# Every tile that a matmul reads begins on a multiple of 128 bytes, on both sides of SBUF

## The chip, the core and the metric

The kernel runs on one core of a Trainium2 chip. The metric is the device time of one execution in microseconds, the median of several runs; lower is better. Engines are named as in the profile: PE (TensorE, matmuls), PEld (TensorE's weight load), DVE (VectorE), ACT (ScalarE), POOL (GpSimd) and SP (SyncE, which here only issues DMAs).

## What is computed

One layer of an encoder block on 512 positions of width 1024, all in float32. The reference, cut to the core:

```python
n = rms_norm(h, norm_mix_pre[l])
proj = jnp.einsum('bsd,de->bse', n, w_in[l])
z_gmlp, q, k, v, gates = jnp.split(proj, split_points, axis=-1)
y_a = gmlp_spatial_gating(jax.nn.gelu(z_gmlp), ln_v_gain[l], ln_v_bias[l], w_spatial[l], b_spatial[l])
...
o_g, lse_g = dilated_window_attention(q[:, :, sl], k[:, :, sl], v[:, :, sl], dilation, window // (2 * dilation))
...
y_b = jnp.sum(w_mix[..., None] * o_all, axis=0).reshape(B, S, ATTN_GROUP_WIDTH).astype(h.dtype)
g_all = jax.nn.sigmoid((gates + b_gate[l]).astype(jnp.float32)).astype(h.dtype)
merged = (g_a * jnp.einsum('bse,ed->bsd', y_a, w_branch_a[l])
          + g_b * jnp.einsum('bse,ed->bsd', y_b, w_branch_b[l]))
h = h + rms_norm(jnp.einsum('bsd,de->bse', merged, w_out[l]), norm_mix_post[l])
n2 = rms_norm(h, norm_mlp_pre[l])
hid = jnp.square(jax.nn.relu(jnp.einsum('bsd,df->bsf', n2, w_up[l])))
h = h + rms_norm(jnp.einsum('bsf,fd->bsd', hid, w_down[l]), norm_mlp_post[l])
```

The widths: q, k and v have 12 heads of 128 each (three groups of four heads), the gMLP part 2 x 512, the gates 2 x 1024, the hidden layer 4096.

## The kernel before

**Precision.** Almost every product is made of three matmuls. Each float32 operand is split into a rounded part `hi` (type float32r, written by ACT) and the rest `lo` (written by DVE), and `mm3` (lines 83 to 87) adds hi times hi, hi times lo and lo times hi in PSUM. Line 85 is the first of the three, 86 the second, 87 the third. The profile shows float32r as f32. The matmuls that are plain float32 are few: transposes, the scores of groups 1 and 2 (line 307), the values of groups 1 and 2 (line 407), the spatial gating (line 472) and some small ones.

**Operands.** A matmul has a stationary operand, 128 columns loaded beforehand by an LDWEIGHTS (PEld), and a moving operand of up to 512 columns that streams past it. The call is `matmul(out, stationary, moving)`. The profile prints "out<-moving,stationary" or the two in the other order, as the names sort.

**Stages, in order of time.** Norm of x and its transposes into `nh`, `nl` (right side); v of group 0 and of groups 1 and 2 (pv, `token_major`; for groups 1 and 2 the stationary operand takes every fourth position of `nh`); for each of four heads the projections of q and k (pf, `feature_tile`, weights stationary, `nh` and `nl` moving), rotary positions, scores and softmax, and the attention of the head before; the gMLP branch (pv and pf again); the gates and the two branch projections (pf; moving `nh`, `nl`, `yah`, `yal`, `ybh`, `ybl`); the output projection (pd; stationary `mh`, `ml`, moving the weights); post-norm, second norm and transposes; the up projection, whose first four feature tiles are plain (pu) and whose others are made of seven products of half size (line 680, 256 columns; moving `n2` tiles, stationary `hl` and `a12` tiles); the down projection (pd; stationary `hh`, `hl` or, for the last four of 32 steps, `hhl`; moving the weights in `hl` of the pool wback); post-norm and output.

The order of the instructions on each engine is made by the framework's scheduler from the program. All weights come by DMA from SP's queue; POOL's queue has small loads and the residual.

**Where tiles lie.** SBUF has 128 partitions, and a tile takes a range of bytes in each. Pools are stacks: those with no side grow upward from the low end, those with `side="right"` grow downward from the high end. A tile starts at the next multiple of 32 bytes behind the tile before it, so odd sizes shift all that comes behind. The addresses of the kernel before, from its allocation (bytes per partition):

| tiles | read by matmuls as | first address | past a multiple of 128 |
|---|---|---|---|
| ident | moving, in transposes | 16512 | 0 |
| onesq | stationary, 3 products in all | 17184 | 32 |
| small tiles xa, xc | moving, 2 small products a head | 18624, 19456 | 64; 0 and 64 |
| hi, lo of weights (wpool, w0pool, gapool, wopool) | both | 44736 ... | 64 |
| v0h, v0l, v12, mh, ml, hl, a12, hh, ptah, ptal, ptb | both | 69312 ... | 64 |
| perm | stationary | 137920 | 64 |
| q1, k1, q2, k2, q0h, q0l, k0h, k0l (apool, behind perm) | both | 138976 ... | 96 |
| nh, nl | both | 192480, 210912 | 96 |
| ybh, ybl, yah, yal | moving | 159712 ... | 96 |
| n2, hhl (n2pool) | moving; stationary | 172000 ... | 96 |

The slices that matmuls take of these tiles begin at multiples of 512 bytes (256 for `nh` and `nl`) from the tile's start, so a slice has its tile's offset. The exceptions are the slices with a step of four positions (lines 212 to 218), which start up to 12 bytes later.

The offsets on the low side come from the pool `consts` (lines 50 to 61): `ident` 512 bytes, `cols` 128, `neghalf` 8 in a place of 32, `onesq` 512, `warm` 8 in a place of 32, together 1216, which is 64 more than a multiple of 128. The pool `small` behind it takes a multiple of 128. The high end of the right side is 229344, 96 more than a multiple of 128, and `nl` ends there. `perm` has 264 columns, 1056 bytes, 32 more than a multiple of 128.

Of the kernel before, what the change touches and what calls it, by code (L numbers as in the profile page):

```python
# [10 lines left out]
F32 = mybir.dt.float32  # L11
# [5 lines left out]
P = 128  # L17
# [19 lines left out]
def block_kernel(ctx: ExitStack, tc: tile.TileContext, x, norm_mix_pre, w_in, b_gate, ln_v_gain, ln_v_bias,  # L37
                 w_spatial, b_spatial, w_branch_a, w_branch_b, w_out, norm_mix_post, norm_mlp_pre, w_up,
                 w_down, norm_mlp_post, ident_c, rope_c, mask_c, perm_c, out):
    nc = tc.nc  # L40
# [3 lines left out]
    def pool(stack, name, bufs=1, space=None, side=None):  # L44
        kw = {"side": side} if side else {}
        if space is not None:
            kw["space"] = space
        return stack.enter_context(tc.tile_pool(name=name, bufs=bufs, reuse_waits="tile", **kw))

    consts = pool(ctx, "consts")  # L50
# [2 lines left out]
    wpool = pool(wstack, "wpool", bufs=3)  # L53

    ident = consts.tile([P, P], F32, name="ident")
    cols = consts.tile([P, 32], F32, name="cols")
    neghalf = consts.tile([P, 2], F32, name="neghalf")
    onesq = consts.tile([P, P], F32, name="onesq")
    nc.vector.memset(onesq, 1.0)
# [29 lines left out]
    def rstd_of(ss, mult, eps=EPS):  # L89
# [7 lines left out]
        nc.gpsimd.tensor_tensor(r, t, neghalf[:, :1], op=ALU.pow)  # L97
        return r

    right = ExitStack()  # L100
    npool = pool(right, "npool", side="right")
    nh = npool.tile([P, KD, S + ROT], F32R, name="nh")
# [130 lines left out]
    apool = pool(proj, "apool")  # L233
# [1 line left out]
    masks = apool.tile([P, 6, P], F32, name="masks")  # L235
    nc.gpsimd.dma_start(rope, rope_c.rearrange("a p s -> p a s"))
    nc.gpsimd.dma_start(masks, mask_c.rearrange("m p c -> p m c"))
    perm = apool.tile([P, 2 * P + 8], F32, name="perm")
    nc.gpsimd.dma_start(perm, perm_c)
    by_r = perm[:, 2 * P:2 * P + 4].unsqueeze(1).unsqueeze(1)  # L240
    by_c = perm[:, 2 * P + 4:2 * P + 8].unsqueeze(1).unsqueeze(3)

# [185 lines left out]
    nc.gpsimd.dma_start(wsp, w_spatial.rearrange("g t s -> t g s"))  # L428
    pt = psA.tile([P, 32], F32, name="ptr", tag="T")
    nc.tensor.transpose(pt, rows, ident[:32, :32])  # L430
    nc.vector.tensor_copy(cols, pt)
    wst = gpool.tile([P, 4, P], F32, name="wst")
    pt = psA.tile([P, 4, P], F32, name="pt", tag="T")
    for g in range(4):
# [2 lines left out]
    pt = psA.tile([P, 4, P], F32, name="prs", tag="T")  # L437
# [135 lines left out]
    for t in range(4):  # L573
# [14 lines left out]
        for q, hs in enumerate(halves):  # L588
            nc.scalar.activation(xn[:, hs], h2[:, hs], AF.Copy, scale=r)
            pt = psB.tile([P, 4, P], F32, name="pt2", tag="tp", bufs=4)  # L590
# [216 lines left out]
```

## Time and profile before

| | us |
|---|---|
| median of 3 runs | 839.2 |
| lowest and highest | 838.79, 840.05 |
| the profiled execution | 839.99 |
| its span, first to last instruction | 838.2 |

The profile shows one execution. A line of its list of groups reads: source line, engine, operation, output tile, input tiles, shapes and count, then busy time in us and mean duration of one in ns, then idle time of the engine just before these and what ended it. Matmuls are pipelined: the duration of one reaches into the next, so their sum is more than the time that passed, and the distance from one start to the next is the cost of one in a stream. A table of stretches gives for each window its length, the busy time and count of the instructions that run in it (those that began before it too), the clock granted to TensorE, the DMA engines' busy share and GB/s. In the timeline the first column is the start from the beginning of the span, the second the duration, both in us.

### The profile page before, as it was taken

To read this page: it belongs to the slowest core of one execution; us is meant where nothing else is said; L and a number is where in the kernel's file an instruction comes from. 1 tells how busy PE (TensorE), PEld (TensorE's weight loads), DVE (VectorE), ACT (ScalarE), POOL (GpSimd) and SP (SyncE) were. 2 spreads that over 40 slices of the span, in tenths; PEclk is the share of its full clock that TensorE was granted. 3 is DMA by queue.
4 is the path that set the end of the run, shared out by engine and by line. 5 is a ranking of instruction groups with operands and counts; after the bars stand their busy time and mean duration, and the time that the engine had idled before them with its cause. 6 is when DMAs were issued, how large, how long until landed. Compare 5 with 4: busy or idle time off the path is not lost.

```text
span 838.2 us, 10932 instructions
## 1 busy us (share of the span) xinstructions
PE 819.9 (98%) x4371; PEld 707.3 (84%) x4371; DVE 491.4 (59%) x831; ACT 348.6 (42%) x561; POOL 84.5 (10%) x78
## 2 busy tenths in 40 slices
PE   7999999999999999999999989999999999999997
PEld 5899888888888778888888879999999888888885
DVE  6422788978764737443333489989887633333324
ACT  6322243444344444323312465666666632223311
POOL 2100113223224300000000220000000100000000
PEclk9999999999999999999999989999999999999999
DMA  9432233231213233422413242334333722222202
GB/s 295 141 101 79 73 101 101 58 93 55 97 51 90 88 100 126 152 77 74 151 51 100 76 154 73 102 109 132 113 101 126 251 99 87 84 87 97 100 1 100
DMA packets 70373, 86.90 MB, mean 104 GB/s; under 512 B 2034, under 2 KB 57490, under 8 KB 70323
## 3 DMA queue, kind: packets, MB, share of 16 engines
q1 hardware_dynamic: 67810, 77.67, 29.5%
q0 software_dynamic: 2512, 8.54, 3.0%
q8 instruction: 34, 0.56, 0.3%
q14 instruction: 17, 0.13, 0.0%
HBM read 82.01 MB, written 4.19 MB: 103 GB/s over the span
## 4 chain that ended last, share of the span: by engine, by line
PE 96%; ACT 2%; DMA 1%; DVE 1%; issue 0%; SPq 0%; DVEq 0%; POOLq 0%; ACTq 0%
PE pf L87 12%; PE pf L86 12%; PE pf L85 12%; PE pacc L680 11%; PE pd L85 9%; PE pd L86 9%; PE pd L87 9%; PE ptp L680 5%; PE pv L85 4%; PE pv L87 4%; PE pv L86 4%; PE pu L85 1%; PE pu L86 1%; PE pu L87 1%; PE py L407 1%; PE psb L307 1%
## 5 line engine op out<-in xcount | busy, mean ns | idle before, releaser
L87 PE MATMUL pf<-nh,lo 128*128 128x512 f32 x352 | 139.9, 397 | 0.0
L86 PE MATMUL pf<-nl,hi 128*128 128x512 f32 x352 | 139.7, 397 | 0.0
L85 PE MATMUL pf<-nh,hi 128*128 128x512 f32 x352 | 139.5, 397 | 0.0
L680 PE MATMUL pacc<-n,hl 128*128 128x256 f32 x840 | 104.4, 279 | 0.0
L680 PEld LDWEIGHTS pacc<-n,hl 128*128 128x128 f32 x840 | 100.9, 188 | 0.2 <-ACT hl L80 0.2
L85 PE MATMUL pd<-hl,hh 128*128 128x512 f32 x224 | 87.1, 390 | 1.0 <-ACT hh L80 1.0
L86 PE MATMUL pd<-hl,hh 128*128 128x512 f32 x224 | 87.2, 389 | 0.0
L87 PE MATMUL pd<-hl 128*128 128x512 f32 x224 | 86.0, 389 | 0.0
L87 PEld LDWEIGHTS pf<-nh,lo 128*128 128x128 f32 x352 | 66.1, 188 | 15.4 <-issue 0.2
L85 PEld LDWEIGHTS pf<-nh,hi 128*128 128x128 f32 x352 | 66.1, 188 | 15.3 <-issue 0.2
L86 PEld LDWEIGHTS pf<-nl,hi 128*128 128x128 f32 x352 | 66.1, 188 | 15.2
L81 DVE TENSOR_TENSOR hl<-hid,hh 128x512 fp32r<-128x512 f32 x28 | 19.3, 693 | 80.4 <-ACT hh L80 78.9
L248 POOL TENSOR_TENSOR sw<-sw,rope 32x512 f32<-32x512 f32 x24 | 43.9, 1830 | 178.6 <-DVE sw L246 161.2
L80 ACT ACTIVATE hh<-hid 128x512 fp32r<-128x512 f32 x28 | 17.6, 631 | 93.3 <-PE pd L86 93.3
L85 PE MATMUL pv<-hi,nh 128*128 128x512 f32 x128 | 52.0, 410 | 1.1 <-ACT nh L80 1.1
L86 PE MATMUL pv<-lo,nh 128*128 128x512 f32 x128 | 51.9, 405 | 0.0
L87 PE MATMUL pv<-hi,nl 128*128 128x512 f32 x128 | 51.9, 407 | 0.0
L85 PEld LDWEIGHTS pd<-hl,hh 128*128 128x128 f32 x224 | 42.0, 188 | 10.4 <-ACT hh L80 1.4
L87 PEld LDWEIGHTS pd<-hl 128*128 128x128 f32 x224 | 42.0, 188 | 8.7
L86 PEld LDWEIGHTS pd<-hl,hh 128*128 128x128 f32 x224 | 42.0, 188 | 8.6
L97 POOL TENSOR_TENSOR rs_out<-rs_in,neghalf 128x1 f32<-128x1 f32 x20 | 14.7, 734 | 333.7 <-DVE rs_in L94 329.9
L81 DVE TENSOR_TENSOR hl<-dnw,hl 128x1024 fp32r<-128x1024 f32 x32 | 39.2, 1226 | 14.0 <-ACT hl L80 14.0
(243 smaller groups left out, 1568.0 us busy)
## 6 DMA issues: line engine op xcount, KB each, us to landing
upw<-in_w_up_dram SPq DMA_DIRECT2D x16, 1024.0 KB, 5.6
dnw<-in_w_down_dram SPq DMA_DIRECT2D x16, 1024.0 KB, 5.0
qkw<-in_w_in_dram SPq DMA_DIRECT2D x24, 512.0 KB, 4.2
gw<-in_w_in_dram SPq DMA_DIRECT2D x8, 1024.0 KB, 5.2
slab<-in_w_in_dram SPq DMA_DIRECT2D x6, 1024.0 KB, 14.0
wow<-in_w_out_dram SPq DMA_DIRECT2D x4, 1024.0 KB, 4.9
w0raw<-in_w_in_dram SPq DMA_DIRECT2D x4, 512.0 KB, 7.1
uw<-in_w_in_dram SPq DMA_DIRECT2D x2, 1024.0 KB, 5.0
```

Of the source, the lines that this page charges most:

```text
L80: nc.scalar.activation(hi, src, AF.Copy)
L81: nc.vector.tensor_tensor(lo, src, hi.bitcast(F32), op=ALU.subtract)
L85: nc.tensor.matmul(ps, ah, bh, start=start, stop=False)
L86: nc.tensor.matmul(ps, ah, bl, start=False, stop=False)
L87: nc.tensor.matmul(ps, al, bh, start=False, stop=stop)
L97: nc.gpsimd.tensor_tensor(r, t, neghalf[:, :1], op=ALU.pow)
L248: nc.gpsimd.tensor_tensor(sw, sw, rope[:, 1], op=ALU.mult)
L307: nc.tensor.matmul(ps[:, rr, g - 1], got["q", g][:, r], got["k", g][:, r], start=True, stop=True)
L407: nc.tensor.matmul(o, v12[:, g, r, hs], ptb[r // 2][:, r % 2, g], start=False, stop=(r == 3 and g == 1), skip_group_check=True)
L680: nc.tensor.matmul(ps, a[:, j], b[:, j], start=first and not (j or m), stop=(j == KH - 1 and m == 2), skip_group_check=True)
```

## The change

Three allocations get another size, and one is new:

- `cols` in consts takes 48 columns instead of 32 (192 bytes instead of 128); the copy that fills it writes its first 32 columns as before.
- `edge`, 24 columns (96 bytes), is allocated first on the right side and set to zero by POOL. Nothing reads it.
- `perm` takes 384 columns (1536 bytes) instead of 264; the DMA that fills it writes its first 264 columns as before.

With the sizes above, `consts` comes to 1280 bytes, ten times 128, `nl` ends 96 bytes lower, on a multiple of 128, and what lies behind `perm` in its pool starts on one. Two things that matmuls read do not: `onesq`, which is then 96 past a multiple of 128, and of the small tiles `xc` by its two buffers of 64 bytes.

```diff
-    cols = consts.tile([P, 32], F32, name="cols")
+    cols = consts.tile([P, 48], F32, name="cols")
...
+    edge = pool(ctx, "edge", side="right").tile([P, 24], F32, name="edge")
+    nc.gpsimd.memset(edge, 0.0)
     right = ExitStack()
...
-    perm = apool.tile([P, 2 * P + 8], F32, name="perm")
-    nc.gpsimd.dma_start(perm, perm_c)
+    perm = apool.tile([P, 3 * P], F32, name="perm")
+    nc.gpsimd.dma_start(perm[:, :2 * P + 8], perm_c)
...
-    nc.vector.tensor_copy(cols, pt)
+    nc.vector.tensor_copy(cols[:, :32], pt)
```

## The prediction, made before the changed kernel had run

> **What bounds the kernel now.** The page comes first: its head, its slices and its chain of waits.
>
> ```profile
> span 838.2 us, 10932 instructions
> PE 819.9 (98%) x4371; PEld 707.3 (84%) x4371; DVE 491.4 (59%) x831; ACT 348.6 (42%) x561; POOL 84.5 (10%) x78
> ...
> PEclk9999999999999999999999989999999999999999
> ...
> PE 96%; ACT 2%; DMA 1%; DVE 1%; issue 0%; SPq 0%; DVEq 0%; POOLq 0%; ACTq 0%
> ```
>
> TensorE is busy for 98% of the span, the records grant it its full clock, and the chain that ends last is 96% PE. So the time is the sum of the distances from one matmul's start to the next one's, and a change counts as far as it changes these. The edits add one memset and move addresses; everything else is whether an address changes a distance.
>
> The list of groups by line and form gives the counts (the number behind x; the groups of lines 85, 86 and 87 stand in equal numbers, so one of three is shown).
>
> ```profile
> L87 PE MATMUL pf<-nh,lo 128*128 128x512 f32 x352 | 139.9, 397 | 0.0
> L680 PE MATMUL pacc<-n,hl 128*128 128x256 f32 x840 | 104.4, 279 | 0.0
> L85 PE MATMUL pd<-hl,hh 128*128 128x512 f32 x224 | 87.1, 390 | 1.0 <-ACT hh L80 1.0
> L85 PE MATMUL pv<-hi,nh 128*128 128x512 f32 x128 | 52.0, 410 | 1.1 <-ACT nh L80 1.1
> L85 PE MATMUL pd<-hi,mh 128*128 128x512 f32 x64 | 24.9, 390 | 0.0
> L680 PE MATMUL ptp<-n,hl 128*128 128x256 f32 x168 | 24.5, 280 | 0.2 <-ACT hl L80 0.2
> L680 PE MATMUL ptp<-n,a12h 128*128 128x256 f32 x112 | 20.3, 279 | 0.0
> L85 PE MATMUL pu<-n,hl 128*128 128x256 f32 x64 | 19.4, 302 | 1.7 <-ACT hl L80 1.7
> L680 PE MATMUL ptp<-n,a12l 128*128 128x256 f32 x56 | 15.6, 279 | 0.0
> L85 PE MATMUL pf<-ybh,hi 128*128 128x512 f32 x32 | 12.7, 398 | 1.2 <-ACT hi L75 1.2
> L85 PE MATMUL pf<-yah,hi 128*128 128x512 f32 x32 | 12.7, 398 | 0.0
> L85 PE MATMUL pd<-hl,hhl 128*128 128x512 f32 x32 | 12.7, 395 | 0.0
> ```
>
> All these are 512 or 256 columns of fp32r, yet the 512-column ones do not agree: 397 ns for pf, 390 for pd. These durations overlap, so the distances are read from the table of stretches (PE alone: length, busy time and matmuls, clock, DMA share, GB/s).
>
> ```profile
> 366.00:432.00 66.00, 66.00 (x285) 1.00 0.29 96
> 670.00:800.00 130.00, 130.00 (x575) 1.00 0.26 89
> 809.40:830.00 20.60, 20.60 (x90) 1.00 0.15 55
> 560.00:640.00 80.00, 80.00 (x688) 1.00 0.35 106
> ```
>
> No stretch has an idle PE. Two of each count were already running at its left edge, so the distances are 66.00/283 = 0.2332, 130.00/573 = 0.2269, 20.60/88 = 0.2341 and 80.00/686 = 0.1166 us. The PE timeline refines the first two (start and duration in us): six distances between the rows of each pair.
>
> ```profile
> 99.73 0.40 PE L85 MATMUL pf<-nh,hi 128*128 128x512 f32 x1
> ...
> 101.13 0.40 PE L85 MATMUL pf<-nh,hi 128*128 128x512 f32 x1
> ```
>
> ```profile
> 700.05 0.39 PE L85 MATMUL pd<-hl,hh 128*128 128x512 f32 x1
> ...
> 701.41 0.39 PE L85 MATMUL pd<-hl,hh 128*128 128x512 f32 x1
> ```
>
> 1.40/6 = 233.3 ns and 1.36/6 = 226.7 ns. The code's addresses go with them. In the down stage (670 to 800) both operands start 64 bytes past a multiple of 128: 226.7. In pf the moving operand nh lies on the right side, 96 past, the stationary one 64 past: 233.3. From 809 us on it is the reverse, moving hl 64 past, stationary hhl 96 past: the third stretch again gives about 233. the stage of seven products (line 680) has moving 96, stationary 64, and 116.6 for 256 columns, half of 233.3.
>
> What would remain without any such cost? Early in the trace the same instruction runs at half its later rate (nine distances):
>
> ```profile
> 11.10 0.63 PE L86 MATMUL pv<-lo,nh 128*128 128x512 f32 x1
> ...
> 14.94 0.63 PE L86 MATMUL pv<-lo,nh 128*128 128x512 f32 x1
> ```
>
> 3.84/9 = 426.7 ns; half is 213.3 for 512 columns, 106.7 for 256. I take these as the bare stream (an estimate: it assumes that the slow rate hides the offset's cost). Over it lie 13.3 ns at 64 and 64, and 20.0 at 64 and 96, for either operand at 96. A simple reading is **a cost per operand**: 6.7 ns per 512 columns for one at 64, 13.3 for one at 96 (a multiple of 32 only). It makes a claim that can be tried here: 256 columns with both at 96 should take 106.7 + 13.3 = 120.0. The scores of group 0 (k0h, q0h) are such a case, on the left side (eight distances):
>
> ```profile
> 129.63 0.28 PE L87 MATMUL psa<-k0h,q0l 128*128 128x256 f32 x1
> ...
> 130.59 0.28 PE L87 MATMUL psa<-k0h,q0l 128*128 128x256 f32 x1
> ```
>
> 0.96/8 = 120.0 ns. So it is the offset and not the side. What no fp32r row shows is an operand at 0. The only operand on a multiple of 128 that matmuls read is ident, in transposes (mean durations 272 and 276 ns for 128 columns; the second moves ptb, at 64):
>
> ```profile
> L378 PE MATMUL pt<-ident,p 128*128 128x128 f32 x32 | 5.3, 272 | 0.0
> ...
> L407 PE MATMUL py<-ptb,v 128*128 128x128 f32 x64 | 8.3, 276 | 0.0
> ```
>
> 4 ns less with it, but a transpose is another kind of pass, so this is a hint only.
>
> **The change part by part.** *cols to 48 columns*: 64 more bytes in consts, so every pool above it on the left, weights, values, merge, hl, goes from 64 to 0. Its copy still writes 32 columns. *perm to 384 columns*: the apool tiles behind it (q, k) go from 96 to 0; its DMA moves the same bytes. *edge*: 96 bytes on the right, so nh, nl, ybh, yah, n2 and hhl go from 96 to 0; its memset joins POOL's queue, whose like takes 0.10 us and whose first work that anyone waits for starts at 6.01:
>
> ```profile
> 0.74 0.10 POOL L60 MEMSET neghalf<- 128x2 f32 x1 [0.29 <-POOLq L796]
> 6.01 0.56 POOL L97 TENSOR_TENSOR rs_out<-rs_in,neghalf 128x1 f32<-128x1 f32 x1 [5.18 <-DVE rs_in L94]
> ```
>
> The 5.18 us of waiting cover it; without them it would be 0.1 us. No wait is added, no DMA and no queue is passed.
>
> *The distances.* Counts from the rows: 64/64 with 512 columns, 3 x (224 + 64) = 864. 64/96, 3 x (352 + 32 + 32 + 32 + 128) = 1728, of which 192 read nh with a step of four columns (lines 212 to 218). 256 columns, 840 + 168 + 112 + 56 + 3 x 64 = 1368. The unknown is what is left at 0/0. Nearest rows as bounds:
> - Lower: the bare stream, 213.3 and 106.7. Saved: 864 x 13.3 = 11.5, 1728 x 20.0 = 34.6, 1368 x 10.0 = 13.7, together 59.8 us.
> - Upper: no better than 64/64 for 512 columns, and 120.0 as in the 96/96 row for 256: 1728 x 6.7 = 11.5 saved, 1368 x 3.3 = 4.6 lost, together 6.9 us saved.
> - Taken: the cost halves with each doubling of alignment (13.3 at 32, 6.7 at 64, 3.3 at 128), which keeps nearest to the two steps that the rows show: 220.0 and 110.0. Saved: 864 x 6.7 = 5.8, 1728 x 13.3 = 23.0, 1368 x 6.7 = 9.1, together 37.9; with nothing left it would be 59.8. I take 44, somewhat past the halving, since the hint of ident points to nothing left.
>
> *What is late next.* In the stage of line 680 DVE comes close (PE, PEld, DVE, ACT busy):
>
> ```profile
> 520.00:650.00 130.00, 129.79 (x1108) 129.43 (x1107) 111.13 (x159) 84.20 (x118) 0.58 (x1) 1.00 0.36 110
> ```
>
> With 7 to 10 ns off 1108 matmuls it becomes 119 to 122 us long against 111 us of DVE: 91 to 93% instead of 85%, so some of its waits surface. Elsewhere DVE and ACT have more room, and the 18 us in which PE idles (838.2 - 819.9) stay. I give back 3 us. Sum: 838.2 - 44 + 3 = 797.2 us of span; the profiled execution took 839.99, 1.8 more than its span, and the median is 0.8 below it: 798.
>
> The Trainium skill, "TensorE: Matmul & The Clock Gate", section "Wait — 56ns, not 53.3ns?", puts back-to-back matmuls at N / 2.4 GHz + 2.5 ns, 215.8 for 512; an estimate by that page is 2.5 ns above my lower bound, and the rows of before stand 10.9 and 17.5 above it. By it the saving would be 9.4 + 30.2 + 10.3 = 49.9 us.
>
> **The rivals.** *64 is already as good as 128* (0.25). The 13.3 ns at 64/64 are then a cost of each fp32r matmul, and only the right side and q, k gain. For it: no row shows less than 226.7. Against it: the costs of the two operands add up in the 120.0 row. Saved: 11.5 us on 512 columns, on 256 between 4.6 more and 4.6 less: 823 to 832, middle 828.
>
> *Nothing changes* (0.10): what distinguishes the groups is something other than the offset, such as which banks they fill or what runs beside them: 839. Against it: pd at 226.7 and at 233.3 is the same line with other stationary tiles. The Trainium skill, "SBUF — State Buffer", section "Specifications (TRN2)", speaks for this: it gives cachelines of 16 bytes, and all the tiles concerned start on a multiple of 32 already, so by it no distance would change and the time would be 839; the rows at 226.7 and 233.3 speak against it.
>
> *Equal offsets collide* (0.09, slower). Two streams that start at the same offset get in each other's way: 120.0 at 96/96 against 116.6 at 96/64 can be read so, and after the change all pairs are equal. Place: line 680 and pu, 1368 x 3.3 = 4.6 us: 844. It decides only where the 512-column ones do not fall in return, that is from less than 2.7 ns each on 1728; 64/64 at 226.7 speaks against it.
>
> **How the numbers follow.** The forecast, a gain past the level of 64/64, has 0.56, and its own range is 782 (59.8 saved, 3 given back) to 810 (37.9 saved, twice as much given back, and some more for the strided ones); the first rival 0.25, the others 0.10 and 0.09. Left out may be 0.2: the range goes from 782 to 834, the upper end of the first rival with 2 us for other waits. Faster by over 0.2% (what a measurement of this kernel can tell from no change) 0.81, within it 0.10, slower 0.09.
>
> **What would show it.** PE counts: at the forecast the stretch of pf has 220 ns or less from start to start, the down stage falls below 226.7, line 680 to 110 or less. If down stays at 226.7 and pf comes to it, it was the first rival. If line 680 goes to 120, equal offsets collide. If DVE becomes the releaser of idle time on PE around 520 to 650 us, I gave back too little. A different order of instructions on PE would make the whole sum wrong.

## The result, and the profile after

The changed kernel takes 841.83 us (median of 16 runs) against 840.12 us for the kernel before, measured beside it (16 runs): a ratio of 1.0022, with a 95% interval from 1.0014 to 1.0031. It is slower by about 0.2%, where 798 us and a range of 782 to 834 had been forecast.

The head of the page after, with its slices of TensorE's clock and its chain:

```profile
span 840.6 us, 10933 instructions
...
PE 822.9 (98%) x4371; PEld 712.1 (85%) x4371; DVE 491.9 (59%) x831; ACT 348.5 (41%) x561; POOL 84.2 (10%) x79
...
PEclk9999999999999999999999989999999999999999
...
PE 96%; ACT 2%; DMA 1%; DVE 1%; issue 0%; SPq 0%; DVEq 0%; POOLq 0%; ACTq 0%
```

Only TensorE's time has changed to speak of: the counts are the same, its 4371 matmuls run in the same order, POOL has one memset more, and the chain has the same shares. The busy time of PE grew by 3.0 us, the span by 2.4. The table of stretches of the kernel after (PE alone), to be laid beside the four rows of before (x285, x575, x90, x688):

```profile
366.00:432.00 66.00, 66.00 (x286) 1.00 0.28 96
670.00:800.00 130.00, 130.00 (x575) 1.00 0.28 96
809.40:830.00 20.60, 20.60 (x91) 1.00 0.14 52
560.00:640.00 80.00, 80.00 (x669) 1.00 0.35 106
```

The first three stretches hold almost the same number of matmuls: pf, the down projection and its last steps run as before. The fourth holds 19 fewer: 80.00/667 = 119.9 ns from start to start instead of 116.6. That is line 680 of before, line 682 after, and the list of groups shows it too:

```profile
L682 PE MATMUL pacc<-n,hl 128*128 128x256 f32 x840 | 106.9, 284 | 0.0
```

against 104.4 us and 279 ns before. The distances were averaged over all starts in the trace, by group, without those over 265 ns (512 columns) or 130 ns (256 columns), which are waits. Times the counts, the changes from before to after are: line 680 from 116.86 to 119.75 ns, +3.4 us; pu from 117.78 to 118.65, +0.2; the products with a step of four positions from 237.70 to 239.82, +0.4; pf from 233.25 to 232.62, -0.8; all others together -0.3. The sum is +3.0 us.

### The profile page after: what moved, and what is told of

Same layout as the page of the kernel before. It is cut to its first block, busy times and chain, and to the rows that moved or that the text cites. A ratio compares the mean times of both kernels' runs of the same rounds, so it can differ in the third digit from the quotient of the medians.

```text
span 840.6 us, 10933 instructions
## 1 busy us (share of the span) xinstructions
PE 822.9 (98%) x4371; PEld 712.1 (85%) x4371; DVE 491.9 (59%) x831; ACT 348.5 (41%) x561; POOL 84.2 (10%) x79
## 4 chain that ended last, share of the span: by engine, by line
PE 96%; ACT 2%; DMA 1%; DVE 1%; issue 0%; SPq 0%; DVEq 0%; POOLq 0%; ACTq 0%
PE pf L87 12%; PE pf L86 12%; PE pf L85 12%; PE pacc L682 11%; PE pd L85 9%; PE pd L87 9%; PE pd L86 9%; PE ptp L682 5%; PE pv L85 4%; PE pv L86 4%; PE pv L87 4%; PE pu L85 1%; PE pu L87 1%; PE pu L86 1%; PE py L409 1%; PE psb L309 1%
## 5 line engine op out<-in xcount | busy, mean ns | idle before, releaser
L682 PE MATMUL pacc<-n,hl 128*128 128x256 f32 x840 | 106.9, 284 | 0.0
L682 PEld LDWEIGHTS pacc<-n,hl 128*128 128x128 f32 x840 | 103.3, 190 | 0.2
```

The source lines that it names most:

```text
L682: nc.tensor.matmul(ps, a[:, j], b[:, j], start=first and not (j or m), stop=(j == KH - 1 and m == 2), skip_group_check=True)
```

## The experiments

Two kinds of kernels were run: the changed kernel with other paddings, and streams of matmuls alone, whose operands lie at chosen addresses. "Offset" is the start of a tile's range past a multiple of 128 or 256 bytes.

**A map of places and offsets.** A kernel of its own, without the layer:

```diff
+    def group(i, j, om, os, ncol, n=24):
+        for k in range(n):
+            a = st[j][:, os + 128 * (k % 2):os + 128 * (k % 2) + 128]
+            b = mv[i][:, om + 512 * (k % 2):om + 512 * (k % 2) + ncol]
+            nc.tensor.matmul(acc[:, 0, :ncol], a, b, start=True, stop=True)
```

> Matmuls alone: it leaves out all of the layer and streams groups of 24 fp32r matmuls, each group with its own place of the moving and of the stationary operand (eight places from 17 KB to 216 KB, all on a multiple of 128), then with offsets of 0, 32, 64, 96 bytes for each, for 512 and for 256 columns. If the side matters (my theory for pf at 232 and the down stage at 226.7): 226.7 ns from start to start with both operands low, about 232 with one high and one low, with a step at one address. If the offset matters alone (the forecast's reading): no dependence on the place, and a dependence on the offset of each. If equal offsets collide: within the grid of offsets the diagonal is the slowest for 256 columns, 120 against 116.7.

The place does not matter. All 64 pairs of eight places (the first moving tile starts at 20.5 KB, the last at 216 KB), at offset 0 and 512 columns, have a mean of 226.65 to 226.70 ns, low with low, low with high, and high with high. So a side theory, formed from pf at 232 and the down projection at 226.7 after the change, fell. The offsets do matter (mean distance in ns from the starts in the trace, without the first three of each group, both operands near 50 KB; the pair of 216 KB and 48 KB gave the same within 1.2):

```
512 columns      stationary 0      32      64      96
moving  0             226.7   233.4   233.4   234.4
moving 32             233.5   226.7   233.3   233.4
moving 64             228.9   233.4   226.7   233.4
moving 96             233.2   228.8   233.3   226.7

256 columns      stationary 0      32      64      96
moving  0             119.7   118.3   117.8   117.3
moving 32             117.8   120.0   118.1   113.4
moving 64             117.8   116.7   119.8   118.3
moving 96             120.0   117.7   117.9   119.7
```

The diagonal is flat, from 0 to 96. No operand has a cost of its own; what counts is the offset of one against the other. Equal offsets are the best case for 512 columns and nearly the worst for 256. With 256 columns the difference does not say all: with the stationary operand 64 past the moving one the map has 117.8 (0 and 64) and 113.4 (32 and 96). The forecast's cost per operand is refuted by the diagonal. Every group writes the same tile in PSUM, and from 20 to 630 us of this trace no engine but TensorE works and the DMA share is 0.00, so neither banks nor neighbours make these differences.

**One side at a time.** From the changed kernel, the low side put back, or the right side:

```diff
-    cols = consts.tile([P, 48], F32, name="cols")
+    cols = consts.tile([P, 32], F32, name="cols")
...
-    perm = apool.tile([P, 3 * P], F32, name="perm")
+    perm = apool.tile([P, 2 * P + 8], F32, name="perm")
```

> Only the right side moves (low 64, right 0; q and k at 96). If equal offsets collide: line 680 at 116.7 ns or less, no loss against before, 839 to 840 us. If a right side at 0 is bad by itself: line 680 at 120 and the time of the full change. If offset costs add up by operand: both fall.

```diff
-    edge = pool(ctx, "edge", side="right").tile([P, 24], F32, name="edge")
-    nc.gpsimd.memset(edge, 0.0)
```

> Only the low side and q, k move (low 0, right 96). If equal offsets collide: line 680 at 116.7 or less, no loss. If a low side at 0 is bad by itself: line 680 at 120. If offset costs add up by operand: the down stage and line 680 both below before.

With the right side alone 839.46 us, ratio 0.9991 [0.9975, 1.0008]; with the low side alone 840.53 us, 1.0015 [1.0005, 1.0024]. Line 680 stands at 117.05 and at 118.33 ns, pf at 233.30 and 233.22. No single expectation fits: in neither kernel do line 680 or pf have equal offsets, yet with the low side alone line 680 is slower than the 116.86 of before, and with the right side alone it is no faster. The difference of the offsets has more than two cases.

**All at 64.** From the changed kernel:

```diff
-    cols = consts.tile([P, 48], F32, name="cols")
+    cols = consts.tile([P, 32], F32, name="cols")
...
-    edge = pool(ctx, "edge", side="right").tile([P, 24], F32, name="edge")
+    edge = pool(ctx, "edge", side="right").tile([P, 8], F32, name="edge")
...
-    perm = apool.tile([P, 3 * P], F32, name="perm")
+    perm = apool.tile([P, 2 * P + 32], F32, name="perm")
```

> All tiles at 64: low as before, right side and q, k brought to 64. If equal offsets collide: as the full change, line 680 at 120 and pf at 232.5, about 842. If 0 is bad by itself: no loss against before. If the offset costs add up by operand (64 better than 96): pf falls to 226.7 and the time by 10 us or more.

834.18 us, ratio 0.9934 [0.9917, 0.9950]. Here pf falls to 227.32 ns, and line 680 rises to 119.97. Each of the three theories has one half right and one wrong. It raises the question of the whole case: all tiles at 64 do what all tiles on 128 were to do, and those on 128 do not. The addresses answer it. With all at 64, nh and the weights both lie 192 past a multiple of 256. After the change the weights lie on a multiple of 256, but nh is at 192384, 128 past one.

**The difference, to 512 bytes.** Matmuls alone again, the stationary operand shifted by 16 bytes at a time:

```diff
+    shifts = [4 * i for i in range(32)] + [1, 2]
+    for ncol in (512, 256):
+        group(0, ncol)
+        for os in shifts:
+            group(os, ncol)
```

> Matmuls alone again (the layer is left out): groups of 36 fp32r matmuls in the order hi hi lo, the moving operand fixed, the stationary one shifted by 0 to 496 bytes in steps of 16, and by 4 and 8, for 512 and for 256 columns. If only the difference of the two offsets modulo 128 counts: the pattern repeats every 128 bytes, 226.7 ns at 0, 128, 256 and 384 for 512 columns and 120 there for 256. If it counts modulo 256: 226.7 at 0 and 256 alone, about 232.5 at 128 and 384, which is what pf shows in the changed kernel (nh is at 128 past a multiple of 256, the weights at 0). If absolute offsets count, 4 and 8 bytes make a step.

The pattern repeats every 256 bytes, within 0.2 ns in all 16 pairs for both widths. Eight of the sixteen steps (ns; the difference is stationary minus moving, modulo 256):

```
difference        0     32     64     96    128    160    192    224
512 columns   226.7  233.4  233.3  234.4  233.5  233.4  228.9  233.3
256 columns   120.0  118.3  113.3  118.7  118.7  120.1  117.8  116.8
```

At 16 and at 240 the 512-column distance is 226.7 as well; shifts of 4 and 8 bytes cost more than one of 16 (232.5 and 230.7 for 512 columns). Some stretches of this kernel's trace (PE), for differences of 0 and 128 at 512 columns and of 0 and 64 at 256:

```profile
153.00:160.00 7.00, 7.00 (x33) 1.00 0.00 0
...
220.00:227.00 7.00, 7.00 (x31) 1.00 0.00 0
...
375.50:379.00 3.50, 3.50 (x31) 1.00 0.00 0
392.50:396.00 3.50, 3.50 (x34) 1.00 0.00 0
```

In equal time 33 against 31 matmuls, and 31 against 34: the difference that serves 512 columns best serves 256 columns worst.

**Multiples of 256.** One number of the change:

```diff
-    edge = pool(ctx, "edge", side="right").tile([P, 24], F32, name="edge")
+    edge = pool(ctx, "edge", side="right").tile([P, 56], F32, name="edge")
```

> The changed kernel with edge at 56 columns instead of 24, so that the right side too begins on multiples of 256. If the difference modulo 256 counts: pf from 232.6 to about 227.3, the hhl matmuls to 226.7, line 680 stays at 120, the time as with all tiles at 64, 834 us (8 less than the change). If the difference modulo 128 counts or if 0 itself is bad and 64 good: as the change, 842.

833.98 us, ratio 0.9929 [0.9913, 0.9946]: pf at 227.42, hhl at 226.66, line 680 at 119.97, all as the difference modulo 256 says. The stretches of before, pf first and line 680 second:

```profile
366.00:426.00 60.00, 60.00 (x259) 1.00 0.32 106
560.00:630.00 70.00, 70.00 (x602) 1.00 0.36 106
```

and of this kernel, where pf goes to 267 and line 680 (line 682 here) to 586:

```profile
366.00:426.00 60.00, 60.00 (x267) 1.00 0.31 106
560.00:630.00 70.00, 70.00 (x586) 1.00 0.36 108
```

**Line 680 by itself.** Now only the n2 tiles move, away from equality; the padding of the kernel just shown closes with nh:

```diff
-    edge = pool(ctx, "edge", side="right").tile([P, 56], F32, name="edge")
-    nc.gpsimd.memset(edge, 0.0)
     right = ExitStack()
+    pool(right, "edge", side="right").tile([P, 56], F32, name="edge")
...
+    pool(back, "edge2", side="right").tile([P, 8], F32, name="edge2")
     n2pool = pool(back, "n2pool", bufs=14, side="right")
```

> All at 0 modulo 256 as in the run before it, but the n2 tiles (and hhl, which shares their pool) at 192, so that in line 680 the stationary operand stands 64 past the moving one. If the difference modulo 256 counts: line 680 at 113.3 ns or, in its other regime of the run with the edge alone, 117.7, instead of 120.0; 1368 x 6.7 or 2.3 ns, so 825 or 831 us, against 834; hhl from 226.7 to about 229. If line 680 is held at 120 by the weight load or by DVE: 834.

With 48 columns in `edge2` instead of 8:

> The same with the n2 tiles at 32, stationary 224 past the moving one, which is the difference that line 680 had before the change. If the difference modulo 256 counts: line 680 back at 116.7 ns, 4.5 us below the run with all at 0 modulo 256, 829.5 us; hhl at about 233. If something else of the change slowed line 680: 120 and 834.

829.58 us (827.10 to 831.26), ratio 0.9887 [0.9867, 0.9907], with line 680 at 113.56; and 830.36 us (830.21 to 831.17), 0.9891 [0.9877, 0.9906], with line 680 at 116.67. The intervals overlap: which of the two is faster is not settled, but both are faster than before by some 9 or 10 us. The 113.56 belongs to the profiled execution of the first one, its fastest, 827.10 us; what line 680 took in its other three, 829.0 to 831.3 us, was not profiled. Its stretch of line 680:

```profile
560.00:630.00 70.00, 70.00 (x620) 1.00 0.35 106
```

620 matmuls instead of 602 (before) or 586. Not all of it reaches the span. The groups of line 680 in this kernel and in the one with everything on 256, from their pages:

```profile
L682 PE MATMUL pacc<-n,hl 128*128 128x256 f32 x840 | 102.0, 277 | 1.2 <-DVE u L704 0.7
```

```profile
L682 PE MATMUL pacc<-n,hl 128*128 128x256 f32 x840 | 106.9, 283 | 0.0
```

The faster stream waits 1.2 us more, 0.7 of it for DVE. Of the 8.8 us saved by 1368 matmuls (119.97 to 113.56), 7.3 reach the span (832.6 to 825.3); the waits take 1.2, and hhl, 2.3 ns slower on 96, takes 0.2.

**All kernels in one table.** The time is the median of the runs; the rest comes from the profiled execution of each: difference modulo 256, measured mean distance, and in brackets the value that the shifts by 16 bytes have for that difference (ns):

| kernel | us | pf | line 680 | hhl |
|---|---|---|---|---|
| before | 839.3 to 840.1 | 224: 233.25 (233.3) | 224: 116.86 (116.8) | 32: 233.28 (233.4) |
| the change | 841.83 | 128: 232.62 (233.5) | 128: 119.75 (118.7) | 128: 232.45 (233.5) |
| right side alone | 839.46 | 64: 233.30 (233.3) | 64: 117.05 (113.3) | 192: 228.94 (228.9) |
| low side alone | 840.53 | 32: 233.22 (233.4) | 32: 118.33 (118.3) | 224: 233.31 (233.3) |
| all at 64 | 834.18 | 0: 227.32 (226.7) | 0: 119.97 (120.0) | 0: 226.67 (226.7) |
| all on 256 | 833.98 | 0: 227.42 (226.7) | 0: 119.97 (120.0) | 0: 226.66 (226.7) |
| n2 at 192 | 829.58 | 0: 227.42 (226.7) | 64: 113.56 (113.3) | 192: 228.92 (228.9) |
| n2 at 32 | 830.36 | 0: 227.41 (226.7) | 224: 116.67 (116.8) | 32: 233.28 (233.4) |

The stage between them, the down projection, has a difference of 0 in all eight and 226.74 to 226.88 ns in all eight. Of 24 cells, 23 lie within 1.1 ns of the value in brackets. The exception, line 680 with the right side alone, has two rates in one execution. The timeline of that kernel (start, duration, and how many were merged):

```profile
537.20 1.52 PE L682 MATMUL pacc<-n,hl 128*128 128x256 f32 x12
...
540.59 0.72 PE L682 MATMUL pacc<-n,hl 128*128 128x256 f32 x4 [0.51 <-ACT hl L80]
541.54 0.51 PE L682 MATMUL ptp<-n,hl 128*128 128x256 f32 x2 [0.22 <-ACT hl L80]
...
543.33 1.93 PE L682 MATMUL pacc<-n,hl 128*128 128x256 f32 x15
```

The last matmul of a merged row takes 0.28 us, the others give the distance: (1.52 - 0.28)/11 = 113 ns before the two short waits for ACT, (1.93 - 0.28)/14 = 118 ns after them, with the same tiles, and it stays near 117.8 to the end of the stage. With a difference of 64 the stream can run at either rate, and here it left the better one at an idle moment. An idle moment alone does not decide it: the kernel with n2 at 192 waits 0.7 and 0.5 us within the stage and goes on at 113. Nor do the addresses alone: at the same ones, offsets 0 and 64 near 50 KB, the first map has 117.8 and the shifts by 16 bytes, whose slices come in another order, 113.3. What decides it was not tried. The ten runs with the right side alone take 835.31 to 840.93 us, three of them under 837; two rates would fit that, but only one run, of 839.62 us, was profiled.

## Why the prediction was wrong

- **What bounds the kernel** was right, and so were the counts and the four distances of before. The sum of the changed distances, +3.0 us, is the growth of PE's busy time; the span grew by 2.4.
- **"A cost per operand" is the step that failed.** The four values 226.7, 233.3, 116.6 and 120.0 were put down to each operand's own offset: 64, 96, 96. They fit the difference of the offsets just as well: 0, 32 either way, and 0. The 120.0, taken for proof of the first reading, fits both.

The trace of before does have a row that tells the two apart, and the step did not use it: the values of group 0 (lines 401 to 403, 256 columns, `v0h` and `v0l` stationary, `ptah` and `ptal` moving), with both operands at 64. The cost per operand gives 106.7 + 3.3 + 3.3 = 113.3 ns, the difference gives the 120.0 of the other equal pair.

```profile
302.21 0.28 PE L403 MATMUL py<-ptah,v0l 128*128 128x256 f32 x1
...
302.69 0.40 PE L86 MATMUL pf<-nl,hi 128*128 128x512 f32 x1
```

Four distances in 0.48 us are 120 ns each. Over the 24 distances between such matmuls without a wait the mean is 119.0.

Modulo 128, the 96 against 96 is also the case that the change makes of line 680. It showed about what line 680 would become, 119.75; modulo 256 the two are not the same, 0 and 128.

- **The bare stream** of 213.3 and 106.7 ns was reached by no alignment tried. Over all the runs here the steady distances go down to 226.65 and 113.3, 17/16 of it. The Trainium skill, "TensorE: Matmul & The Clock Gate", section "Wait — 56ns, not 53.3ns?", by whose formula the prediction estimated 215.8 for 512 columns, is not met by any fp32r stream of these runs.
- **The term of 44 us saved** measured 3.0 us lost. Its three parts: 64/64 at 512 columns, 5.8 to 11.5 forecast, 0.1 measured; 64/96, 23.0 to 34.6 forecast, 0.5 measured; 256 columns, 9.1 to 13.7 forecast, 3.6 lost.
- **DVE coming up in the stage of line 680** had no occasion in the change. In the kernel with n2 at 192, where line 680 does get 6.4 ns faster, it shows as 0.7 us of waiting for DVE and 0.5 for ACT, where 3 us had been given back for 7 to 10 ns.
- **The rival "64 is already as good as 128"** was right on 0 against 0 (226.7 in the map, as 64 against 64) and wrong in what follows for pf, since in the change nh and the weights are not equal but 128 apart modulo 256. The two kernels that make them equal show its gain on 512 columns: pf at 227.3 and 227.4, 834 us.
- **The rival "equal offsets collide"** had the place, the direction and nearly the price: 1368 x 3.3 = 4.6 us, measured 3.6 (844 us forecast, 841.83 measured). Its condition, that the 512-column matmuls do not fall in return, held for a reason it did not have. With truly equal offsets they do fall and outweigh it by far. So it came this close in part by luck: the 3.3 ns are the price of equality, and the change gave line 680 a difference of 128, which happens to cost nearly as much. The argument held against it, 226.7 at 64/64, says nothing about 256 columns. It was given 0.09.
- **The rival "nothing changes"**, 839 us, was off by 0.3%. The Trainium skill, "SBUF — State Buffer", section "Specifications (TRN2)", was cited for it, in that 16-byte lines would leave every distance as it is. With 512 columns a shift of 16 bytes from equality does, 226.7 ns; one of 32 bytes costs 6.7 ns more. Nor was it something else than the offsets: the streams of matmuls alone show the distances with neither banks nor neighbours to tell the groups apart.

The chances followed the wrong reading: 0.81 for faster was the sum of the forecast and its first rival, which both go by each operand's own offset and had no fp32r row at 0. A range that takes in every rival with a place and a price would have reached 844.

## What to carry to other kernels

A variable that fits every row looked at can still be the wrong one: before forecasting from offsets, write each row both by operand and by difference, and look for a row that separates them. In a kernel bound by back-to-back fp32r matmuls, each with a stationary operand of its own as here, place the two operands relative to each other, modulo 256 bytes, and for each shape by itself: equal for 512 moving columns, here 64 or 224 apart for 256. A round number of bytes for all tiles is neither needed nor enough.

## What the runs showed of the hardware

Not expected were these:

- The distance between fp32r matmuls depends on the difference of the two operands' start addresses modulo 256 bytes, not on either address: 226.7 to 234.4 ns for 512 columns, and 226.7 for 64 pairs of places from 20.5 to 216 KB. For 256 columns it goes from 113.3 to 120.1 ns, and the same difference gave values up to 1.4 ns apart in the two streams, more at 64.
- The same difference that is best for 512 columns (0: 226.7) is next to the worst for 256 (120.0).
- At a difference of 64, 256 columns have two rates, 113.3 and 117.8 ns, and one execution changed from the first to the second at a wait of half a microsecond; another passed such a wait without changing.

Open are why it is so, what sets the rate in the last case, and why line 680 has 119.75 ns at a difference of 128 in the kernel where the shifts by 16 bytes have 118.7.
